# Float16 projection tiles of a hybrid decoder block: squares, scale sums and conversions issued a tile apart, and the last two raw tiles interleaved

## The chip, the cores and the metric

The kernel runs on one core of one Trainium2 chip. The metric is the device time of one execution in microseconds. Of the kernel before there are three timed runs, with a median of 2944.93 us, and one profiled execution.

## The reference, cut to what matters

```python
h = rms_norm(x, norm1_g)                 # x: 512 x 2048, float32
z = h @ w_in                             # w_in: 2048 rows; 72 tiles of up to 128 columns
zs = token_shift(z[..., :RW_SHIFT_COLS], rw_mu)
o_rw = rwkv7_mix(zs, ...)                # sequential over 512 tokens, 16 heads
o_att = swa_attention(q, k, v, ...)      # window 128, 16 query heads, 4 key heads
p = g_rw * (o_rw @ w_branch[:RW]) + g_att * (o_att @ w_branch[RW:])
x = x + p @ w_out
x = x + conv_ffn(rms_norm(x, norm2_g), w_up, conv_w, conv_b, w_down)
```

The change lies in `z = h @ w_in` and in what is interleaved with it. The rest, from `w_out` on, is not touched.

## The kernel before, in words

The output z is built transposed, one tile of 128 columns of `w_in` at a time: a tile is a sum over NK = 16 blocks of 128 input features, and each block takes three matmuls of 128x512 (high weight half times high input half, high times low, low times high), so 48 matmuls a tile. There are two kinds of tiles.

- **Raw tiles**, the first NR = 5 (two of keys, two of values, the first of queries). Their operands are float32r halves. `project` (L276) takes the 16 blocks in four groups of four. For each group `load_w` (L265) brings 256 KB of weights by a DMA on the SyncE queue into a tile of pool "raw" (four buffers), ScalarE writes the high half (`whi`, L271) and VectorE the low half (`wlo`, L272), four buffers each. The input halves are `xhi` and `xlo`, four tiles of four blocks each.
- **Float16 tiles**, the other 67. `zload(i)` (L357) brings the whole tile, 1 MB, in two DMAs, into one of four buffers that share their places with the four groups of `xhi` (tag "h1"); so the first four loads have to wait until the last raw tile has read a group for the last time. ScalarE squares each half and sums along the row (L367, output `zsq`, which takes two buffers of the same pool "raw"). `ztotal(i)` (L371) sums these over the partitions by two matmuls with one column each (L378) into the first column of the PSUM bank that tile i will accumulate in, and VectorE turns the sum into a power of two with four or five short instructions (L383 to L390). `zconv(i)` (L392) multiplies by it: ScalarE writes the high float16 half (`whi`, L402, two instructions a tile) and VectorE the low half (`wlo`, L403, two a tile), into the four buffers that the raw tiles use too. The 48 matmuls stand in L422. The float16 input `x16` is written by `row_scaled` (VectorE, L474) and `split` (ScalarE and VectorE, L220 and L221).

`ztile` (L406) puts these together. Before the change, tile i runs its matmuls, with `ztotal(i + 1)` after block 10 of 16; then come `zconv(i + 1)` and `zload(i + 5)`, whose squares are written right behind its DMAs.

Every engine works through its own queue in a fixed order. That order is made when the kernel is built: a list scheduler takes, on each engine, the earliest instruction in program order whose inputs it expects to be ready by its own estimate of durations. `behind(ins, other)` forces one instruction behind another on the same engine, and `pin` behind everything traced on that engine. Around the float16 tiles the program has three stages: attention (up to about 300 us), the start of the RWKV part (to about 405 us), and eight pairs of heads. In each pair the chain in `late(p)` (products of 64x64 blocks in L822 to L929, then eight steps of the scan in L936 to L949) is interleaved with six float16 tiles; `entries` ties some of its matmuls to places in the stream of tile matmuls. After about 1290 us come the products with `w_out`, `w_up` and `w_down` (L1176, L1312).

Of the kernel before, what the change touches and what calls it, by code (L numbers as in the profile page):

```python
# [19 lines left out]
P = 128  # L20
S = 512
# [114 lines left out]
def block_kernel(ctx: ExitStack, tc: tile.TileContext, d: Dims, a: dict, out: bass.AP):  # L136
    nc = tc.nc
    act, dve, pool, pe, sync = nc.scalar, nc.vector, nc.gpsimd, nc.tensor, nc.sync
    NK, NP, NQ, NKV, NF = d.NK, d.NP, d.NQ, d.NKV, d.NF
# [23 lines left out]
    cstp = abc.enter_context(tc.tile_pool(name="cstp", bufs=1))  # L163
    cst = cstp.tile([P, NCONST - P], F32, name="cst")
    mus = cstp.tile([P, 2, P], F32, name="mus")
    ones16 = cstp.tile([P, P], BF16, name="ones16")
    gsc = cstp.tile([P, 3], F32, name="gsc")
    xd = a["x"]
    GF = 4
    big1 = abc.enter_context(tc.tile_pool(name="big1", bufs=NK // GF, reuse_waits="tile"))  # L170
    wp = {"n": 0, "step": 3, "after": {}}
# [6 lines left out]
    x16 = x16p.tile([P, 2, NK, S], F16, name="x16")  # L178
# [4 lines left out]
    XG = 2  # L183
    xT = [px.tile([P, XG, S], F32, name=f"xT{i}") for i in range(NK // XG)]
# [34 lines left out]
    def split(hi, lo, src, pin=free):  # L219
        pin(act.activation(hi, src, AF.Copy))  # L220
        pin(dve.tensor_tensor(lo, src, hi.bitcast(F32) if hi.dtype == F32R else hi, op=ALU.subtract))  # L221
# [6 lines left out]
    for f in range(NPRE):  # L228
        w, t = a["w_up"][f], {n: up_d[f, n] for n in ("s3", "s1", "P6", "P3")}
# [19 lines left out]
    stream = []  # L249

    def behind(ins, before):
        tc.add_manual_dep(ins.ins, before.ins.name,
                          mybir.DependencyInfo(mybir.DependencyClass.NoSync, mybir.DependencyReason.DATA))
# [19 lines left out]
        background()  # L273
        return hi, lo

    def project(acc, src, xhi, xlo, pre=(), then=lambda i: None):  # L276
        nk = src.shape[1]
        for k0 in range(0, nk, 4):
            n = min(4, nk - k0)
            whi, wlo = pre[k0 // 4] if k0 // 4 < len(pre) else load_w(src[:, k0 : k0 + n])  # L280
            for j in range(n):
                k = k0 + j
                first, last = k == 0, k == nk - 1
                stream.append(pe.matmul(acc, whi[:, j], xhi(k), start=first, stop=False))  # L284
                stream.append(pe.matmul(acc, whi[:, j], xlo(k), start=False, stop=False))  # L285
                stream.append(pe.matmul(acc, wlo[:, j], xhi(k), start=False, stop=last))  # L286
            then(k0 // 4)


    id16 = cstp.tile([P, P], F16, name="id16")  # L290
# [6 lines left out]
    if True:  # L297
        xhi, xlo = by_group("xhi", "h1"), by_group("xlo", "l1")
        zt = {c: a["w_z"][i].rearrange("p (k c) -> p k c", c=P) for i, c in enumerate(d.z_tiles())}
# [4 lines left out]
        src = a["xT"].rearrange("p (k s) -> p k s", s=S)  # L304
        first = {d.c_ka: []}
# [27 lines left out]
        accp = pa.enter_context(tc.tile_pool(name="accA", bufs=3, space=PSUM, side="right", reuse_waits="tile"))  # L333

        zs = d.z_tiles()
        NR = 2 * NKV + 1
        at = 2 * NKV + NQ
        lead = at + 2 + d.GL // P + 3
        gated = [d.c_zr + i * P for i in range(2 * NK)]
        seq = zs[:at] + gated[:1] + zs[at:lead]  # L340
# [4 lines left out]
            used += GATES_PER_PAIR * NK // 16  # L345
        seq += gated[used:]
        zn = {"i": 0}
        Z = [{} for _ in seq]

        def mu_col(c0):  # L350
# [6 lines left out]
        def zload(i):  # L357
            if i >= len(seq):
                return
            raw = big1.tile([P, NK, P], F32, name="zraw", tag="h1")  # L360
            sums = cstp.tile([P, 2], F32, name="zsum", tag="zsum", bufs=4)
            Z[i].update(raw=raw, sums=sums)
            for h in range(2):
                ks = slice(h * NK // 2, (h + 1) * NK // 2)
                wp["last"] = sync.dma_start(raw[:, ks], zt[seq[i]][:, ks])
                sq = wp["raw"].tile([P, NK // 2, P], BF16, name="zsq", tag="raw")
                act.activation(sq, raw[:, ks], AF.Square, accum_out=sums[:, h : h + 1])  # L367
                for _ in range(2):
                    background()

        def ztotal(i):  # L371
            if i >= len(seq):
                return
            z = Z[i]
            z["acc"] = acc = accp.tile([P, S], F32, name="acc", tag="acc")
            part = z["sums"].bitcast(BF16)
            for h in range(2):
                ins = pe.matmul(acc[:, 0:1], ones16, part[:, 2 * h + 1 : 2 * h + 2], start=h == 0, stop=h == 1)  # L378
                behind(ins, stream[-1])
            q = cstp.tile([P, 1], I32, name="zq", tag="zq", bufs=2)  # L380
            zc = z["c"] = cstp.tile([P, 4], F32, name="zc", tag="zc", bufs=4)
            scale, back, e = zc[:, 0:1], zc[:, 1:2], zc[:, 2:4]
            dve.tensor_scalar(q, acc[:, 0:1].bitcast(I32), 24, None, op0=ALU.logical_shift_right)  # L383
            dve.tensor_scalar(scale.bitcast(I32), q, -(1 << 23), 204 << 23, op0=ALU.mult, op1=ALU.add)
            dve.tensor_scalar(back.bitcast(I32), q, 1 << 23, 50 << 23, op0=ALU.mult, op1=ALU.add)
            m = mu_col(seq[i])
            if m is not None:
                dve.tensor_scalar(e, mus[:, :, m], back, None, op0=ALU.mult)
            else:
                dve.tensor_scalar(e[:, 0:1], gsc[:, 1:2] if seq[i] < d.c_zr else gsc[:, 2:3], back, None, op0=ALU.mult)  # L390

        def zconv(i):  # L392
            if i >= len(seq):
                return
            z = Z[i]
            scale = z["c"][:, 0:1]
            raw = z.pop("raw")
            z["parts"] = []
            for h in range(2):
                src = raw[:, h * NK // 2 : (h + 1) * NK // 2]  # L400
                hi, lo = (wp["hl"].tile([P, NK // 2, P], F16, name=f"w{e}16", tag=f"w{e}") for e in ("hi", "lo"))
                act.activation(hi, src, AF.Copy, scale=scale)  # L402
                dve.scalar_tensor_tensor(lo, src, scale, hi, op0=ALU.mult, op1=ALU.subtract)  # L403
                z["parts"].append((hi, lo))

        def ztile(c0):  # L406
            i = zn["i"]
            zn["i"] += 1
            assert seq[i] == c0
            if i < NR:  # L410
                acc = accp.tile([P, S], F32, name="acc", tag="acc")
                last = i == NR - 1
                project(acc, zt[c0], xhi, xlo, first.pop(c0, ()), lambda g: zload(NR + g) if last else None)
                if last:
                    ztotal(NR)
            else:
                z = Z[i]
                acc, parts = z["acc"], z.pop("parts")
                for k in range(NK):
                    hi, lo = (x[:, k % (NK // 2)] for x in parts[2 * k // NK])  # L420
                    for w, e in ((hi, 0), (hi, 1), (lo, 0)):
                        stream.append(pe.matmul(acc, w, x16[:, e, k], start=k == 0 and e == 0 and w is hi,  # L422
                                                stop=k == NK - 1 and w is lo))
                    if k == 2 * NK // 3:
                        ztotal(i + 1)
                wp["e"] = z["c"][:, 2:4]
            if i >= NR - 1:
                zconv(i + 1)
                zload(i + 5)
            return acc  # L430

        acc_k = ztile(d.c_ka)
# [5 lines left out]
        with tc.tile_pool(name="x0_ps", bufs=1, space=PSUM) as ps0:  # L438
# [15 lines left out]
            q = p0.tile([P, 1], I32, name="gq")  # L454
# [17 lines left out]
        def row_scaled(k):  # L472
            x = xT[k // XG][:, k % XG]
            dve.scalar_tensor_tensor(x, x, n1s[:, k : k + 1], rowb, op0=ALU.mult, op1=ALU.mult)  # L474

        def scaled_halves():
            for k in range(NK):
                split(x16[:, 0, k], x16[:, 1, k], xT[k // XG][:, k % XG])
            xin.close()
            wp["gate"] = pa.enter_context(tc.tile_pool(name="gate", bufs=1, side="right"))  # L480
            wp["p"] = pt.enter_context(tc.tile_pool(name="attp", bufs=1, side="right", reuse_waits="tile"))
# [30 lines left out]
        with ExitStack() as pt:  # L512
# [59 lines left out]
            for t in range(1, NKV):  # L572
                for c0, then in ((d.c_ka, keys), (d.c_va, values)):
                    acc = ztile(c0 + t * P)
                    if spread:
                        behind(spread.pop(0), stream[-2 * NK - 1])
                        spread.clear()
                    todo.pop()()
                    todo.append(lambda acc=acc, then=then, t=t: then(acc, t))
                    for k in range(NK // 2) if then is keys else range(NK // 2, NK):  # L580
                        row_scaled(k)

            GQ = d.HQ // NHK

# [1088 lines left out]
```

## Time and profile before

| what | value |
|---|---|
| timed runs | 2940.71, 2944.93, 2949.1 us |
| profiled execution, time and span | 2952.12 us, 2950.3 us |
| busy shares of the span | PE 94%, PE weight loads 72%, VectorE 69%, ScalarE 50%, GpSimd 8% |
| mean granted TensorE clock | 0.977 |
| DMA traffic | 623.78 MB, 211 GB/s in the mean |

PE is TensorE's matmul side, PEld its weight load, DVE is VectorE, ACT is ScalarE, POOL is GpSimd, SP is SyncE and SPq its DMA queue. A row of a timeline gives the start in us, the duration in us, engine, line, operation, output and inputs, shapes and count; in square brackets stands how long the engine had been idle before it and what it waited for. A row of the waits gives the waiting engine and line, what it waited for, the total in us, the number of times and the longest. A row of stretches gives the length, then busy time and instructions of each engine, the granted clock, the DMA engines' share and GB/s.

### The profile page before, as it was taken

The page shows a single profiled execution, that of the slowest core. Times are in us where ns is not written, and L with a number is a line of the kernel's source. Part 1 is how long each engine was busy: PE and PEld are TensorE (multiplying, and loading weights), DVE is VectorE, ACT ScalarE, POOL GpSimd, SP SyncE. Part 2 cuts the span into 40 slices and gives each one's busy share as a digit, 9 for nine tenths or more (in the row PEclk, how much of TensorE's full clock was granted, in tenths as well). Part 3 has the DMA queues.
Part 4 walks back from the last instruction along what each step waited for, and adds up shares of the span by engine and source line. Part 5 has one row for each costly group of instructions (what it writes and reads, how often), then busy time and mean ns, then how long its engine had stood idle before and what let it go on. Part 6 is the DMA issues. An engine that isn't in the chain of part 4 may idle for free.

```text
span 2950.3 us, 45754 instructions
## 1 busy us (share of the span) xinstructions
PE 2776.3 (94%) x17547; PEld 2131.7 (72%) x17547; DVE 2034.1 (69%) x3621; ACT 1478.8 (50%) x2379; POOL 231.5 (8%) x309
## 2 busy tenths in 40 slices
PE   7788888988988989999999999999999999999999
PEld 6344345544544545468888999999999999888887
DVE  7378467677677677544567877778778777665555
ACT  6356454464454465432256655555554555544444
POOL 0000101100100100101100001011011110000000
PEclk9899999999999999999999999999999999999999
DMA  5654776866866766757877688888898887877775
GB/s 211 189 134 125 196 193 165 216 177 167 227 171 162 199 158 165 203 172 228 286 246 256 197 222 236 227 229 227 234 242 234 227 227 213 309 241 243 254 257 191
DMA packets 209035, 623.78 MB, mean 211 GB/s; under 512 B 22816, under 2 KB 42928, under 8 KB 207792
## 3 DMA queue, kind: packets, MB, share of 16 engines
q1 hardware_dynamic: 140256, 445.22, 45.2%
q0 software_dynamic: 37216, 136.33, 24.3%
q10 hardware_dynamic: 31344, 39.31, 3.8%
q8 instruction: 137, 2.24, 0.3%
q14 instruction: 82, 0.67, 0.1%
HBM read 571.16 MB, written 191.18 MB: 258 GB/s over the span
## 4 chain that ended last, share of the span: by engine, by line
PE 65%; DVE 12%; DMA 12%; ACT 6%; issue 3%; SPq 1%; POOL 0%; ACTq 0%; POOLq 0%; DVEq 0%
PE X L1312 17%; DMA zraw<-in_w_z_dram 10%; PE X L1176 9%; PE Y L1312 8%; PE Y L1176 8%; PE acc L422 7%; PE Z L1312 4%; DVE wlo L403 3%; PE acc L286 2%; PE acc L284 2%; PE acc L285 2%; ACT zsq L367 2%; ACT whi L402 2%; PE psS L945 1%; PE psG L936 1%
## 5 line engine op out<-in xcount | busy, mean ns | idle before, releaser
L422 PE MATMUL acc<-x,whi 128*128 128x512 f16 x2144 | 684.6, 391 | 25.6 <-ACT whi L402 21.9
L422 PE MATMUL acc<-x,wlo 128*128 128x512 f16 x1072 | 417.0, 389 | 11.7 <-DVE wlo L403 11.7
L1169 DVE TENSOR_TENSOR wlo<-raw,whi 128x1024 fp32r<-128x1024 f32 x210 | 256.7, 1224 | 199.9 <-ACT whi L1168 199.9
L422 PEld LDWEIGHTS <-whi 128*128 128x128 f16 x2144 | 208.4, 102 | 232.8 <-ACT whi L402 31.1
L1168 ACT ACTIVATE whi<-raw 128x1024 fp32r<-128x1024 f32 x210 | 222.6, 1061 | 281.5 <-PE X L1176 146.7
L1295 DVE TENSOR_TENSOR wlo<-raw,whi 128x1024 fp32r<-128x1024 f32 x184 | 224.6, 1222 | 77.7 <-ACT whi L1293 77.7
L1312 PE MATMUL X<-b,whi 128*128 128x256 f32 x1472 | 268.9, 283 | 0.2 <-ACT whi L1293 0.2
L1312 PE MATMUL X<-t,whi 128*128 128x256 f32 x1408 | 257.2, 283 | 1.4 <-ACT u L1340 1.4
L1312 PE MATMUL Y<-t,whi 128*128 128x256 f32 x1408 | 257.1, 283 | 0.0
L367 ACT ACTIVATE zsq<-zraw 128x1024 bf16<-128x1024 f32 x134 | 141.3, 1054 | 195.2 <-DMA zraw<-in_w_z_dram 194.1
L1293 ACT ACTIVATE whi<-a 128x1024 fp32r<-128x1024 f32 x124 | 130.9, 1056 | 200.8 <-DVE a L1288 197.2
L1312 PEld LDWEIGHTS X<-b,whi 128*128 128x128 f32 x1472 | 229.6, 192 | 0.4 <-ACT whi L1293 0.4
L1312 PEld LDWEIGHTS X<-t,whi 128*128 128x128 f32 x1408 | 219.6, 192 | 1.6 <-ACT u L1340 1.6
L1312 PEld LDWEIGHTS Y<-t,whi 128*128 128x128 f32 x1408 | 219.6, 192 | 0.0
L1312 PE MATMUL X<-b,wlo 128*128 128x256 f32 x736 | 208.6, 283 | 0.9 <-DVE wlo L1295 0.9
L422 PEld LDWEIGHTS <-wlo 128*128 128x128 f16 x1072 | 109.1, 102 | 133.3 <-DVE wlo L403 26.8
L403 DVE SCALAR_TENSOR_TENSOR wlo<-zraw,zc,whi 128x1024 f16<-128x1024 f32 x134 | 170.0, 1281 | 50.4 <-ACT whi L402 49.4
L1293 ACT ACTIVATE whi<-raw 128x1024 fp32r<-128x1024 f32 x184 | 193.0, 1049 | 22.8 <-ACT whi L1293 14.7
L1312 PE MATMUL X<-t,wlo 128*128 128x256 f32 x704 | 199.4, 283 | 0.5 <-DVE wlo L1295 0.5
L1312 PE MATMUL Y<-t,wlo 128*128 128x256 f32 x704 | 199.4, 283 | 0.2 <-DVE wlo L1295 0.2
L1295 DVE TENSOR_TENSOR wlo<-a,whi 128x1024 fp32r<-128x1024 f32 x124 | 151.9, 1225 | 67.6 <-ACT whi L1293 67.1
L1176 PE MATMUL X<-wlo,hhi 128*128 128x512 f32 x480 | 187.1, 390 | 0.8 <-DVE wlo L1169 0.8
(424 smaller groups left out, 5956.4 us busy)
## 6 DMA issues: line engine op xcount, KB each, us to landing
raw<-in_w_up_dram SPq DMA_DIRECT2D x170, 512.0 KB, 4.8
zraw<-in_w_z_dram SPq DMA_DIRECT2D x134, 512.0 KB, 5.8
s_dn<-in_w_dn_dram POOLq DMA_DIRECT2D x88, 512.0 KB, 6.4
raw<-s_dn SPq DMA_DIRECT2D x88, 512.0 KB, 3.9
raw<-in_w_up_dram POOLq DMA_DIRECT2D x80, 512.0 KB, 8.2
raw<-in_w_dn_dram SPq DMA_DIRECT2D x66, 512.0 KB, 3.7
s_dn<-in_w_dn_dram SPq DMA_DIRECT2D x44, 512.0 KB, 7.0
s_dn<-s_dn SPq DMA_DIRECT2D x44, 512.0 KB, 6.0
```

The costliest lines, as they stand in the source:

```text
L284: stream.append(pe.matmul(acc, whi[:, j], xhi(k), start=first, stop=False))
L285: stream.append(pe.matmul(acc, whi[:, j], xlo(k), start=False, stop=False))
L286: stream.append(pe.matmul(acc, wlo[:, j], xhi(k), start=False, stop=last))
L367: act.activation(sq, raw[:, ks], AF.Square, accum_out=sums[:, h : h + 1])
L403: dve.scalar_tensor_tensor(lo, src, scale, hi, op0=ALU.mult, op1=ALU.subtract)
L422: stream.append(pe.matmul(acc, w, x16[:, e, k], start=k == 0 and e == 0 and w is hi, stop=k == NK - 1 and w is lo))
L1168: act.activation(whi, wr, AF.Copy)
L1169: dve.tensor_tensor(wlo, wr, whi.bitcast(F32), op=ALU.subtract)
L1176: pe.matmul(dst, l[:, q, ts], r[:, es], start=fst and j == 0, stop=lst and j == 2, skip_group_check=True)
L1293: pin(act.activation(hi, t, AF.Copy))
L1295: return lambda: pin(dve.tensor_tensor(lo, t, hi.bitcast(F32), op=ALU.subtract))
L1312: pin(pe.matmul(ps, l[:, k], r[:, k], start=start and k + i == 0, stop=last and i == 2, skip_group_check=True))
```

## The change

- `zload` only loads. The squares become `zsquare(i)`, which is issued a tile before the sum needs it, and is forced behind the last conversion of the tile before (`behind(ins, after)`).
- `ztotal(i + 2)` comes at block 8 of tile i. Its column is put into the bank that tile i + 1 will accumulate in (column i % 2). `zconv(i + 2)`, then `zsquare(i + 3)` and `zload(i + 5)` follow at the end of tile i. So conversions are two tiles ahead of their matmuls where they were one ahead.
- The last two raw tiles (second value tile and first query tile) run together in `zpair`: group by group, first the one and then the other, and `zload(NR + g)` after group g of both. `zsquare(NR)` follows group 1; the sum and conversion of tile NR and the squares of NR + 1 stand ahead of group 3.
- `x16` is made pair of blocks by pair of blocks (128x1024) right behind `row_scaled`, ahead of those two raw tiles in program order; before it was made block by block behind the first query tile.

```diff
-    def project(acc, src, xhi, xlo, pre=(), then=lambda i: None):
+    def project(acc, src, xhi, xlo, pre=(), at=(0, 1)):
...
-                first, last = k == 0, k == nk - 1
+                first, last = k + at[0] == 0, k == nk - 1 and at[0] == at[1] - 1
...
-            then(k0 // 4)
...
         def zload(i):
...
-            raw = big1.tile([P, NK, P], F32, name="zraw", tag="h1")
-            sums = cstp.tile([P, 2], F32, name="zsum", tag="zsum", bufs=4)
-            Z[i].update(raw=raw, sums=sums)
+            raw = Z[i]["raw"] = big1.tile([P, NK, P], F32, name="zraw", tag="h1")
             for h in range(2):
                 ks = slice(h * NK // 2, (h + 1) * NK // 2)
                 wp["last"] = sync.dma_start(raw[:, ks], zt[seq[i]][:, ks])
-                sq = wp["raw"].tile([P, NK // 2, P], BF16, name="zsq", tag="raw")
-                act.activation(sq, raw[:, ks], AF.Square, accum_out=sums[:, h : h + 1])
                 for _ in range(2):
                     background()
 
-        def ztotal(i):
+        def zsquare(i, after=None):
+            if i >= len(seq):
+                return
+            raw = Z[i]["raw"]
+            sums = Z[i]["sums"] = cstp.tile([P, 2], F32, name="zsum", tag="zsum", bufs=4)
+            for h in range(2):
+                sq = wp["raw"].tile([P, NK // 2, P], BF16, name="zsq", tag="raw")
+                ins = act.activation(sq, raw[:, h * NK // 2 : (h + 1) * NK // 2], AF.Square, accum_out=sums[:, h : h + 1])
+                if after is not None:
+                    behind(ins, after)
+
+        def zacc(i):
+            if "acc" not in Z[i]:
+                Z[i]["acc"] = accp.tile([P, S], F32, name="acc", tag="acc")
+            return Z[i]["acc"]
+
+        def ztotal(i, bank):
...
-            z["acc"] = acc = accp.tile([P, S], F32, name="acc", tag="acc")
-            part = z["sums"].bitcast(BF16)
+            part, tot = z["sums"].bitcast(BF16), zacc(bank)[:, i % 2 : i % 2 + 1]
             for h in range(2):
-                ins = pe.matmul(acc[:, 0:1], ones16, part[:, 2 * h + 1 : 2 * h + 2], start=h == 0, stop=h == 1)
+                ins = pe.matmul(tot, ones16, part[:, 2 * h + 1 : 2 * h + 2], start=h == 0, stop=h == 1)
                 behind(ins, stream[-1])
...
-            dve.tensor_scalar(q, acc[:, 0:1].bitcast(I32), 24, None, op0=ALU.logical_shift_right)
+            dve.tensor_scalar(q, tot.bitcast(I32), 24, None, op0=ALU.logical_shift_right)
...
-                act.activation(hi, src, AF.Copy, scale=scale)
+                ins = act.activation(hi, src, AF.Copy, scale=scale)
                 dve.scalar_tensor_tensor(lo, src, scale, hi, op0=ALU.mult, op1=ALU.subtract)
                 z["parts"].append((hi, lo))
+            return ins
+
+        def zpair(tiles):
+            for g in range(NK // GF):
+                if g == NK // GF - 1:
+                    ztotal(NR, NR)
+                    at = zconv(NR)
+                    zsquare(NR + 1, at)
+                for acc, c0 in tiles:
+                    project(acc, zt[c0][:, g * GF : (g + 1) * GF], lambda k: xhi(g * GF + k), lambda k: xlo(g * GF + k),
+                            at=(g, NK // GF))
+                zload(NR + g)
+                if g == 1:
+                    zsquare(NR)
...
         def ztile(c0):
...
-                last = i == NR - 1
-                project(acc, zt[c0], xhi, xlo, first.pop(c0, ()), lambda g: zload(NR + g) if last else None)
-                if last:
-                    ztotal(NR)
-            else:
-                z = Z[i]
-                acc, parts = z["acc"], z.pop("parts")
-                for k in range(NK):
...
-                    if k == 2 * NK // 3:
-                        ztotal(i + 1)
-                wp["e"] = z["c"][:, 2:4]
-            if i >= NR - 1:
-                zconv(i + 1)
-                zload(i + 5)
+                if i < NR - 2:
+                    project(acc, zt[c0], xhi, xlo, first.pop(c0, ()))
+                else:
+                    held.append((acc, c0))
+                    if len(held) == 2:
+                        zpair(held)
+                return acc
+            if i == NR:
+                zload(NR + 4)
+            acc, parts = zacc(i), Z[i].pop("parts")
+            for k in range(NK):
...
+                if k == NK // 4 and i == NR:
+                    ztotal(NR + 1, NR + 1)
+                    zsquare(NR + 2, zconv(NR + 1))
+                if k == NK // 2:
+                    ztotal(i + 2, i + 1)
+            wp["e"] = Z[i]["c"][:, 2:4]
+            zsquare(i + 3, zconv(i + 2))
+            zload(i + 5)
             return acc
...
         def scaled_halves():
-            for k in range(NK):
-                split(x16[:, 0, k], x16[:, 1, k], xT[k // XG][:, k % XG])
...
                     for k in range(NK // 2) if then is keys else range(NK // 2, NK):
                         row_scaled(k)
+                        if k % XG == XG - 1:
+                            split(*(x16[:, e, k + 1 - XG : k + 1] for e in range(2)), xT[k // XG])
```

More of the change, by code (lines that the diff above doesn't have):

```diff
@@ L347, in block_kernel @@
         zn = {"i": 0}
+        held = []
         Z = [{} for _ in seq]
@@ L411, in ztile @@
                 acc = accp.tile([P, S], F32, name="acc", tag="acc")
-                last = i == NR - 1
-                project(acc, zt[c0], xhi, xlo, first.pop(c0, ()), lambda g: zload(NR + g) if last else None)
-                if last:
-                    ztotal(NR)
-            else:
-                z = Z[i]
-                acc, parts = z["acc"], z.pop("parts")
-                for k in range(NK):
[L420 to L423, printed above, removed]
-                    if k == 2 * NK // 3:
-                        ztotal(i + 1)
-                wp["e"] = z["c"][:, 2:4]
-            if i >= NR - 1:
-                zconv(i + 1)
-                zload(i + 5)
+                if i < NR - 2:
[9 more added lines that the diff above has]
+            for k in range(NK):
+                hi, lo = (x[:, k % (NK // 2)] for x in parts[2 * k // NK])
+                for w, e in ((hi, 0), (hi, 1), (lo, 0)):
+                    stream.append(pe.matmul(acc, w, x16[:, e, k], start=k == 0 and e == 0 and w is hi,
+                                            stop=k == NK - 1 and w is lo))
+                if k == NK // 4 and i == NR:
[6 more added lines that the diff above has]
+            zload(i + 5)
             return acc
```

## The prediction

> **What bounds the kernel now.** I read the page first, then stretches of time cut at the stages, then the waits of each stage, then timelines around the worst of them.
>
> ```profile
> PE 2776.3 (94%) x17547; PEld 2131.7 (72%) x17547; DVE 2034.1 (69%) x3621; ACT 1478.8 (50%) x2379; POOL 231.5 (8%) x309
> ```
>
> ```profile
> 62.00:104.00 42.00, 20.23 (x57) 14.07 (x56) 14.66 (x39) 9.48 (x18) 0.00 (x0) 0.67 0.34 113
> 104.00:135.00 31.00, 27.44 (x120) 11.91 (x120) 14.14 (x45) 12.72 (x19) 3.43 (x4) 0.89 0.86 248
> 135.00:300.00 165.00, 143.69 (x717) 74.42 (x718) 130.27 (x373) 91.54 (x238) 12.98 (x17) 0.97 0.52 139
> 300.00:405.00 105.00, 86.05 (x436) 40.72 (x434) 60.84 (x130) 52.50 (x87) 10.65 (x17) 0.96 0.70 186
> 405.00:1250.00 845.00, 759.46 (x5048) 417.21 (x5046) 587.05 (x1489) 448.18 (x876) 85.17 (x114) 0.96 0.70 185
> 1290.00:1440.00 150.00, 149.62 (x661) 122.75 (x660) 71.31 (x121) 36.58 (x60) 16.00 (x22) 1.00 0.79 238
> ```
>
> PE bounds everything. From 1290 us on it is full (149.6 of 150), and there nothing changes; time can only come out of PE's idle time before that: 21.8 us in 62 to 104, then 3.6, 21.3, 19.0 and 85.5, together 151 us. The waits, first ScalarE's longest of the whole run, then PE's in 300 to 405, then PE's in 405 to 1250:
>
> ```profile
> ACT zsq L367 <- DMA zraw<-in_w_z_dram: 194.1, 92, 11.0
> ```
>
> ```profile
> PE acc L422 <- ACT whi L402: 10.2, 4, 6.5
> PE acc L422 <- DVE wlo L403: 3.6, 6, 0.7
> ```
>
> ```profile
> PE bulk L873 <- DVE XIW L221: 34.2, 25, 3.7
> PE psS L945 <- DVE UV L941: 13.0, 9, 2.7
> PE acc L422 <- ACT whi L402: 8.7, 6, 1.5
> PE bulk L921 <- DVE XIW L917: 7.9, 10, 1.7
> PE acc L422 <- DVE wlo L403: 3.7, 11, 0.6
> ```
>
> ScalarE stood 194.1 us in front of squares whose tile had not landed, with all else in its queue behind them. PE stood in front of conversions (L402, L403) and of results of the chain.
>
> **The start, 50 to 105 us.** PE, SP's queue, ScalarE and PE again, from their timelines:
>
> ```profile
> 64.46 0.39 PE L285 MATMUL acc<-xlo,whi 128*128 128x512 f32 x1
> 64.69 0.39 PE L286 MATMUL acc<-xhi,wlo 128*128 128x512 f32 x1
> ```
>
> ```profile
> 65.11 0.83 SPq L365 DMA_DIRECT2D zraw<-in_w_z_dram  x2
> 66.04 0.36 SPq L268 DMA_DIRECT2D raw<-in_w_z_dram  x1
> ```
>
> ```profile
> 69.40 1.06 ACT L367 ACTIVATE zsq<-zraw 128x1024 bf16<-128x1024 f32 x1 [8.65 <-DMA zraw<-in_w_z_dram]
> ```
>
> ```profile
> 72.82 0.79 PE L284 MATMUL acc<-xhi,whi 128*128 128x512 f32 x1 [1.62 <-ACT whi L271]
> ...
> 105.17 0.60 PE L422 MATMUL acc<-x,whi 128*128 128x512 f16 x2
> ```
>
> The query tile's group 0 ends at 65.1 and its group 1 starts at 72.8: 7.7 us. Its weights were issued (66.04) only behind the tile load that had waited for the group's last read, and converted behind the squares of that load. This recurs at each of its groups. The clock granted in 62 to 104 was 0.67, so after a halt matmuls come about 0.4 us apart instead of 0.23 (64.46 to 64.69). By the Trainium skill ("TensorE: Matmul & The Clock Gate", Part 1) the clock halves after an idle window of some 3.4 us and returns after as much work: about 8 slow matmuls a halt, an estimate of 1.6 us each. By that rule the sum below would change by about 1 us; the 0.67 agrees with its direction.
>
> Interleaved, a group lasts 24 matmuls, 5.5 us, and the squares leave ScalarE's way. Two things stand against a full gain. The first is VectorE (then one row of ScalarE, and the landing time of the weights' DMA):
>
> ```profile
> 43.52 0.74 DVE L474 SCALAR_TENSOR_TENSOR xT<-xT,n1s,rowb 128x512 f32<-128x512 f32 x1
> ...
> 56.03 4.05 DVE L474 SCALAR_TENSOR_TENSOR xT<-xT,n1s,rowb 128x512 f32<-128x512 f32 x6
> 60.01 0.67 DVE L272 TENSOR_TENSOR wlo<-raw,whi 128x512 fp32r<-128x512 f32 x1
> 60.61 1.27 DVE L221 TENSOR_TENSOR x<-xT,x 128x512 f16<-128x512 f32 x2
> ```
>
> ```profile
> 52.52 0.63 ACT L271 ACTIVATE whi<-raw 128x512 fp32r<-128x512 f32 x1 [1.05 <-issue]
> ```
>
> ```profile
> raw<-in_w_z_dram SPq DMA_DIRECT2D x3, 256.0 KB, 5.1
> ```
>
> The `whi` done at 53.2 got its `wlo` only at 60.0: VectorE first took row scalings that stand earlier in the program, and the `x16` halves, which stand later, after it. In the new program all 16 scalings and all 8 paired `x16` low halves stand ahead of the pair's weights. From 43.5: 16 x 0.675 (4.05 / 6) = 10.8, 8 x 1.27 = 10.2, and an estimated 3 for key and value steps between: 67.5, and 0.67 for the delayed `wlo`: 68.2. Only the pair's very first `wlo` is made before the scalings begin. So PE, which starts the pair at about 49.8 (64.9 less 60 x 0.23 and 1.3 of small matmuls), runs one tile's group 0, halts from about 52.6 to 68.2, and ends group 0 with 10 matmuls at 0.4 at 72.3. Group 1, its weights long there: 5.5 and 1 for the clock, 78.8. Group 2: its buffers of pool "raw" are handed out behind the first squares, so its DMA goes out behind the first tile load, as all three did before: issued 73.2, landed 5.1 later, converted in 0.6 + 0.7: 79.6; end 86. Group 3: its buffers come behind the squares of NR + 1, and these behind a conversion behind a sum behind group 2; so its DMA goes out behind the third load: 7.7 us as before, 93.7, and 24 matmuls at a mean of 0.33: 101.6. Tile NR, converted meanwhile, starts there instead of at 105.2: **-4 us**. Best, without any of these halts: 49.8 + 22.1 + 2.6 of small matmuls = 74.5, that is -31. Worst, group 2's weights behind the second load too: 7 later, +3. I take -4, because the rows show buffers and VectorE following program order.
>
> **The float16 tiles.** Per tile there are the same two loads, squares, sums and conversions; only places change:
>
> ```profile
> L367 ACT ACTIVATE zsq<-zraw x134: 1039/1057/1067, 69.4 to 1235.7; 128x1024 bf16<-128x1024 f32 x134
> L367 ACT ACTIVATION_READ_ACCUMULATOR zsq<-zraw x134: 185/186/212, 70.4 to 1236.7; 128x1 f32 x134
> L402 ACT ACTIVATE whi<-zraw,zc x134: 1131/1136/1150, 104.0 to 1280.1; 128x1024 f16<-128x1024 f32 x134
> ```
>
> The squares of tile i + 3 come three tile ends after its load, so ScalarE's 194.1 us should vanish. On SP a load no longer waits for the conversion just ahead of it, and the background copies pinned behind the loads go no later. What late ScalarE and late conversions cost PE, first in the scan, then between a pair's first products:
>
> ```profile
> 589.68 1.06 ACT L367 ACTIVATE zsq<-zraw 128x1024 bf16<-128x1024 f32 x1 [3.87 <-DMA zraw<-in_w_z_dram]
> ```
>
> ```profile
> 591.25 1.12 PE L945 MATMUL psS<-UV,W 128*128 128x64 f32 x4 [2.46 <-DVE UV L941]
> ```
>
> ```profile
> 612.34 0.19 PE L378 MATMUL acc<-zsum,ones 128*128 128x1 bf16 x2
> ```
>
> ```profile
> 621.60 0.14 DVE L383 TENSOR_SCALAR zq<-acc 128x1 int32<-128x1 int32 x1
> ```
>
> ```profile
> 621.73 0.20 PE L873 MATMUL bulk<-XIW,BT 128*128 128x64 f16 x1 [3.04 <-DVE XIW L221]
> ...
> 624.00 1.03 PE L422 MATMUL acc<-x,whi 128*128 128x512 f16 x2 [1.51 <-ACT whi L402]
> ```
>
> Before 591 the scan waited for a copy that ScalarE could not make while it stood in front of a load. At 612.3 a sum was done, but VectorE, full of chain work, read it 9.3 us later; PE had neither chain nor tile.
>
> - 104 to 135: of 3.6 us idle those for conversions, and some of the slow clock (0.89): -3 (0 to -5).
> - 135 to 300, attention: 21.3 idle, most of it on the chain, which is freed from ScalarE's stalls in part: -5 (0 to -11).
> - 300 to 405: conversions 10.2 + 3.6 = 13.8 of 19.0, made a tile earlier now: -12 (0 to -16, with the clock).
> - 405 to 1250: conversions 8.7 + 3.7 = 12.4, of which -11. Scan 13.0: -10. Level products 34.2 + 7.9 = 42.1: halts like the 3.04 at 621.73, one in each of seven pairs, 21 us, stay, because the sum of tile i + 2 now sits in the bank of tile i + 1 and bars its first matmul until VectorE has read it; of the other 21 half, -10. Slow clock behind halts (two matmuls in 1.03 at 624.0): -2. Together -33 (0 to -50).
> - behind 1250, the last conversions: -2 (0 to -3).
>
> **New waits.** The sum of tile i + 2 needs squares that stand behind a conversion, which needs a buffer that PE frees at the end of tile i - 1. From there ScalarE needs 1.14 + 2 x (1.06 + 0.19) = 3.6 us; half a tile is 24 matmuls at 0.22 or so, 5.2. The slack is 1.6 us; chain work in ScalarE's queue can eat it, and then PE, in order, stands at the sum, with the chain's matmuls behind it. No row shows this wait; the nearest is PE's for ScalarE's conversions, 8.7 us. I take +8, with 0 and 67 tiles x 1.5 = 100 as ends.
>
> Sum: -4 - 3 - 5 - 12 - 33 - 2 + 8 = **-51 us** from the profiled execution's 2952.1 (span 2950.3): 2901. The median of the runs is 7.2 lower: **2894 us**. A difference of 0.3%, 9 us, is about what a measurement of this kernel can tell from none.
>
> **Rivals.**
> - *The start works in full.* If the pair's weights are there in time after all, it ends near 78 instead of 101.6: 2894 - 23 = 2871. For it: ScalarE and the DMA engines have room in 62 to 104 (9.48 of 42 us, a share of 0.34). Against: the `wlo` at 60.01.
> - *It doesn't do what it says.* The wait for the conversion is replaced by that for the bank: tiles start when VectorE has read the next sum, as late as at 621.60. Then the conversions' 25 and some 4 of clock and tail stay, and the start is at its bad end (+7): 2894 + 36, and with a reshuffled chain about 2935. For it: the 9.3 us behind 612.34. Against: the read is one short VectorE step, where the conversion needs three more on two engines.
> - *Slower: PE stands at the sums*, the wait of the last paragraph, in 67 tiles. It decides from (51 + 8) / 67 = 0.9 us a tile, that is with ScalarE 2.5 us late; at 1.5 it is 2894 - 8 + 100 = 2986. For it: the slack of 1.6. Against: the sum is placed where the squares are expected, and ScalarE is busy 448 of 845 us.
>
> **The numbers.** Forecast 0.55 (own range 2870 to 2920), full start 0.18, no real gain 0.15, slower 0.12. Faster: the first two, a third of the third and a little of the last, 0.79; same 0.09; slower 0.12. The range leaves out the slower case and the tails of the others: 2858 to 2945.
>
> **What would show it.** Right: no square waiting for `zraw`; L402 and L403 gone from PE's waits; scan waits (L945) under 4 us; PE idle in the pairs near 60 instead of 85.5; at the start one halt of some 15 us after the pair's first 12 matmuls and one of 8 ahead of its last group; the 3 us halts at L873 still there. Wrong: PE waiting at L378 for `zsum`, or at L422 for VectorE's L383, or a start without halts.

## The result, and the profile after

The changed kernel takes 2863.4 us (median of four runs, 2860.6 to 2869.3) where the kernel before took 2942.8 beside it: a ratio of 0.973 (95% interval 0.9707 to 0.9754), 79 us faster. The forecast was 2894 with a range of 2858 to 2945. Sign and mechanism came as forecast, the size was half as large again. The experiments below show that one of the four things that the change does earns nearly all of it, and that another one costs time.

The page after, first part, and its windows, cut at the same events as the windows of the kernel before that follow: the first float16 matmul, the first attention score product, the first product of the first pair's chain (L822 before, L852 after), the last float16 matmul. The columns are length, busy time of each engine, granted clock, DMA share.

```profile
PE 2747.2 (96%) x17547; PEld 2129.0 (74%) x17547; DVE 2032.1 (71%) x3613; ACT 1470.3 (51%) x2371; POOL 231.0 (8%) x309
```

```profile
50.00:96.00 46.00, 24.41 (x89) 18.60 (x88) 22.76 (x55) 12.76 (x17) 0.00 (x0) 0.74 0.27 83
96.00:145.50 49.50, 46.10 (x207) 23.45 (x207) 24.45 (x76) 20.68 (x31) 5.04 (x6) 0.90 0.97 279
145.50:350.40 204.90, 194.08 (x984) 98.14 (x984) 164.44 (x440) 127.17 (x292) 21.99 (x32) 0.99 0.65 182
350.40:1204.80 854.40, 795.92 (x5331) 443.71 (x5332) 626.35 (x1562) 474.10 (x932) 88.14 (x118) 0.98 0.71 189
```

```profile
50.00:105.20 55.20, 33.30 (x125) 25.09 (x124) 26.46 (x64) 18.92 (x33) 0.00 (x0) 0.75 0.30 97
105.20:146.90 41.70, 37.77 (x169) 16.22 (x169) 20.61 (x66) 16.17 (x23) 4.23 (x5) 0.92 0.84 245
146.90:378.10 231.20, 198.14 (x971) 99.01 (x971) 162.40 (x435) 122.67 (x285) 20.86 (x31) 0.96 0.58 156
378.10:1292.20 914.10, 819.44 (x5347) 445.60 (x5346) 630.21 (x1570) 482.94 (x935) 89.75 (x121) 0.96 0.68 180
```

The spans fell from 2950.3 to 2862.0, by 88.3 (the profiled execution before was 9 us above its median). Up to the first score product the gain is 1.4 us (146.9 to 145.5), from there to the chain 26.3, in the pairs 59.7, and behind them 1. PE did nearly the same number of matmuls in the pairs (5347 and 5331), yet its busy time fell by 23.5 us: they ran less often at the slow clock (0.96 to 0.98). The other 36 us there are idle time, 94.7 to 58.5.

The longest waits of PE up to 1230 us, after:

```profile
PE acc L450 <- DVE zq L394: 23.8, 9, 3.1
PE acc L284 <- ACT whi L271: 15.8, 3, 7.8
PE mi L528 <- DVE rq L211: 13.6, 6, 10.3
PE bulk L903 <- DVE XIW L221: 6.0, 18, 0.5
...
PE psS L975 <- DVE UV L971: 4.7, 21, 0.3
...
PE acc L389 <- ACT zsq L374: 2.4, 2, 2.1
```

The waits for conversions are down to two at the very start of tile NR (1.7 and 0.7 us), the scan's wait fell from 13.0 to 4.7, and ScalarE's wait for `zraw`, 194.1 us before, is down to one of 0.4. Its first square stood longer, but the profile names another DMA for it:

```profile
ACT zsq L374 <- DMA zraw<-in_w_z_dram: 0.4, 1, 0.4
```

```profile
79.13 1.06 ACT L374 ACTIVATE zsq<-zraw 128x1024 bf16<-128x1024 f32 x1 [11.86 <-DMA kd<-kn]
```

The load of that square's tile went out only at 74.00 (below), so a part of these 11.9 us can be a wait for it. There are two such waits, 16.9 us in all, both before 125 us; in the pairs no square waits for a load.

New at the top is PE's wait for `zq`, VectorE's reading of a sum: the halt of 3.1 us, in seven of the eight pairs, that stood at L873 before, now at the tile's own first matmul. PE, then VectorE, in the third pair:

```profile
557.77 0.19 PE L389 MATMUL acc<-zsum,ones 128*128 128x1 bf16 x2
...
572.87 1.01 PE L450 MATMUL acc<-x,whi 128*128 128x512 f16 x2 [3.09 <-DVE zq L394]
```

```profile
568.09 0.68 DVE L878 TENSOR_TENSOR BT<-AI,cst 128x512 f16<-128x512 f16 x1
...
572.68 0.14 DVE L394 TENSOR_SCALAR zq<-acc 128x1 int32<-128x1 int32 x1
```

The sum was done at 558; VectorE got to it at 572.68, behind a stretch of the chain's level work, and until then the next tile may not write its bank. At the start, PE's halts and then SP's queue:

```profile
68.74 0.38 PE L528 MATMUL mi<-ident,rq 128*8 128x128 f32 x1 [10.35 <-DVE rq L211]
...
86.08 0.80 PE L284 MATMUL acc<-xhi,whi 128*128 128x512 f32 x1 [6.89 <-ACT whi L271]
```

```profile
74.00 6.02 SPq L363 DMA_DIRECT2D zraw<-in_w_z_dram  x4
80.12 0.85 SPq L268 DMA_DIRECT2D raw<-in_w_z_dram  x2
```

VectorE's order holds the pair up as forecast, and the third group's weights go out behind two whole tile loads, not one.

### The profile page after: what moved, and what is told of

It is laid out like the page before. It is cut to its first block, busy times and chain, and to the rows that moved or that the text cites. A ratio compares the mean times of both kernels' runs of the same rounds, so it can differ in the third digit from the quotient of the medians.

```text
span 2862.0 us, 45787 instructions
## 1 busy us (share of the span) xinstructions
PE 2747.2 (96%) x17547; PEld 2129.0 (74%) x17547; DVE 2032.1 (71%) x3613; ACT 1470.3 (51%) x2371; POOL 231.0 (8%) x309
## 4 chain that ended last, share of the span: by engine, by line
PE 70%; DVE 15%; ACT 7%; DMA 5%; issue 3%; SPq 0%; POOL 0%; ACTq 0%; DVEq 0%; POOLq 0%
PE X L1342 17%; PE X L1206 10%; PE acc L450 9%; PE Y L1342 9%; PE Y L1206 9%; PE Z L1342 4%; DVE wlo L414 2%; PE acc L286 2%; PE acc L284 2%; PE acc L285 2%; ACT whi L413 2%; ACT zsq L374 2%; PE psS L975 1%; PE psG L966 1%; DVE tt L919 1%
## 5 line engine op out<-in xcount | busy, mean ns | idle before, releaser
L450 PE MATMUL acc<-x,whi 128*128 128x512 f16 x2144 | 664.5, 385 | 25.5 <-DVE zq L394 23.8
L450 PE MATMUL acc<-x,wlo 128*128 128x512 f16 x1072 | 412.2, 385 | 0.7 <-DVE wlo L414 0.7
L450 PEld LDWEIGHTS <-whi 128*128 128x128 f16 x2144 | 207.4, 100 | 231.9 <-issue 44.4
L413 ACT ACTIVATE whi<-zraw,zc 128x1024 f16<-128x1024 f32 x134 | 153.1, 1146 | 130.7 <-PE acc L450 61.2
L1323 ACT ACTIVATE whi<-raw 128x1024 fp32r<-128x1024 f32 x184 | 192.9, 1049 | 23.1 <-ACT whi L1323 13.9
L450 PEld LDWEIGHTS <-wlo 128*128 128x128 f16 x1072 | 108.3, 101 | 112.9 <-issue 12.3
```

The lines of the kernel that those rows point to most:

```text
L413: ins = act.activation(hi, src, AF.Copy, scale=scale)
L1323: pin(act.activation(hi, t, AF.Copy))
```

## The experiments

Theory at the outset: the gain comes from squares and conversions both being further apart, and the interleaved pair helps the start. Rival A: the squares' place alone is the loss. All versions beside the kernel before, median and ratio with interval; "first" is the time of the first float16 matmul, "per pair" the mean distance of two pairs' first chain products.

| version | us | ratio | first | per pair |
|---|---|---|---|---|
| before | 2942 to 2948 | 1 | 105.2 | 109.9 |
| changed | 2863.4 | 0.9730 (0.9707, 0.9754) | 96.0 | 102.9 |
| e1 squares apart only | 2846.0 | 0.9666 (0.9651, 0.9681) | 75.9 | 102.2 |
| e2 sums and conversions only | 2933.3 | 0.9958 (0.9944, 0.9973) | 104.7 | 109.3 |
| e3 both, no pair | 2839.7 | 0.9643 (0.9628, 0.9659) | 75.7 | 102.8 |
| e4 changed, `x16` halves behind | 2858.1 | 0.9707 (0.9692, 0.9722) | 88.9 | 102.6 |
| e5 changed, early sums | 2821.6 | 0.9578 (0.9548, 0.9607) | 94.0 | 100.3 |
| e6 = e3, early sums | 2803.0 | 0.9524 (0.9498, 0.9549) | 76.0 | 100.2 |
| e7 before, first four squares moved | 2914.1 | 0.9903 (0.9874, 0.9932) | 81.4 | 109.0 |
| e8 = e4, pair's weights ahead | 2846.4 | 0.9667 (0.9637, 0.9698) | 88.0 | 102.6 |
| e9 = e1, early sums | 2807.9 | 0.9543 (0.9517, 0.9568) | 75.7 | 101.4 |
| e10 = e6, squares not tied | 2884.5 | 0.9796 (0.9765, 0.9828) | 76.0 | 111.6 |

**e1, the squares apart, nothing else.** Sum and conversion stay one tile ahead, raw tiles and `x16` as before.

```diff
-                sq = ...; act.activation(sq, raw[:, ks], AF.Square, ...)     # in zload
+            at = zconv(i + 1)
+            zsquare(i + 3, at)          # behind the conversion; the first behind the last raw tile
             zload(i + 5)
```

> The kernel before with one part of the change: squares tied behind conversions and issued two tiles after their load; sums and conversions stay one tile ahead, raw tiles and x16 as before. My theory (both parts are needed, each for other waits): ScalarE's 194 us in front of zraw go, with them PE's scan waits (13.0 us) and half of the level waits; the conversion waits (33 us over the run) and the halt at the start of each pair stay, so also the slow clock behind it: some -35 us, about 2908. Rival A (squares waiting for DMAs were the whole loss): near the changed kernel, 2863 to 2875. Rival B (the distance of the conversions is the whole gain): 2935 to 2945.

2846.0: alone it earns 99 us, more than the whole change. The theory (about 2908) fell, and the time lies even below the 2863 to 2875 of Rival A. ScalarE's waits from 50 to 1300, the first two and that for `zraw`, of which 7.2 us are left, and then its start on SP's queue:

```profile
ACT UV L954 <- PE psU L953: 107.2, 48, 4.3
ACT whi L409 <- DVE zc L391: 90.9, 43, 6.7
...
ACT zsq L374 <- DMA zraw<-in_w_z_dram: 7.2, 1, 7.2
```

```profile
38.84 13.78 SPq L268 DMA_DIRECT2D raw<-in_w_z_dram  x7
...
65.17 3.52 SPq L363 DMA_DIRECT2D zraw<-in_w_z_dram  x4
```

The raw weights all go out before the first tile load. Before, the last three groups went out right behind tile loads (66.04 behind 65.11, 79.35 behind 78.44, 91.27 behind 90.38). With the squares written behind the raw tile, PE goes from 50 to 75.9 (25.9 us instead of 55.2) with one halt, of 1.9 us at its end, and with no interleaving at all. The place of the squares decides this: in e7 below, which moves nothing else, the raw weights go out first too. Whether the shared buffers of pool "raw" or the scheduler's estimates held them back was not tested.

**e2, sums and conversions two tiles ahead, squares at the loads.**

```diff
-                    if k == 2 * NK // 3:
-                        ztotal(i + 1)
+                    if k == NK // 2:
+                        ztotal(i + 2, i + 1)
...
-                zconv(i + 1)
+                zconv(i + 2)
```

> The kernel before with the other part: sums and conversions two tiles ahead, with the sum in the next tile's bank; squares stay right behind their DMAs, raw tiles and x16 as before. My theory: the conversion waits go and are partly replaced by waits for VectorE's read of the sum (about 3 us a pair), while ScalarE still stands in front of zraw (over 150 us) and the scan waits stay near 13: some -35 us, about 2908. Rival A: 2935 to 2945. Rival B: 2863 to 2875.

2933.3, 12 us, nearest to Rival A (2935 to 2945). ScalarE still stands, and the per-pair span hardly moves:

```profile
ACT zsq L367 <- DMA zraw<-in_w_z_dram: 184.3, 87, 10.1
```

The first chain product comes at 365.3 instead of 378.1: the 12.8 us are those of the stretch ahead of the chain. So the theory (about 2908) falls in this half too, and the squares' place is nearly the whole loss.

**e3, both, without the pair and with `x16` where it was.**

```diff
-                else:
-                    held.append((acc, c0))
-                    if len(held) == 2:
-                        zpair(held)          # project one after the other again, zload(NR + g) in the last
```

> Both parts of e1 and e2 together, without the interleaved pair and with x16 where it was. My theory: the pair and the moved x16 brought only about 1 us, since a halt of 16 us behind the delayed low half ate what the interleaving saved; so this is within 8 us of the changed kernel, 2855 to 2871, and the gains of e1 and e2 add up to it or to more. Rival (the pair carries a part of the gain): 10 to 25 us slower than the changed kernel, 2875 to 2890.

2839.7, 24 us faster than the changed kernel, outside what either side expected: the interleaved pair, with the moved `x16` halves, is a loss. First float16 matmul at 75.7 instead of 96.0, and the first score product at 114.5 instead of 145.5. Of that lead of 31.0 us 23.1 are left at the first chain product (327.3 against 350.4).

**e4, the changed kernel with the `x16` halves behind the first query tile again.**

```diff
         def scaled_halves():
+            for i in range(NK // XG):
+                split(*(x16[:, e, i * XG : (i + 1) * XG] for e in range(2)), xT[i])
```

> The changed kernel with the x16 halves written behind the first query tile again (still in pairs of blocks). My theory: the halt of 16 us after the pair's first 12 matmuls came from VectorE taking the x16 halves and scalings first. Without the halves ahead, the second tile's low half comes some 10 us earlier; the halts of 7 us in front of groups 2 and 4 stay: 8 to 12 us faster than the changed kernel, about 2853. Rival (the halt is the weights' DMA or ScalarE): no difference, 2860 to 2867.

2858.1: 5 us, between the theory (8 to 12) and the rival (none), and the intervals of the two ratios overlap. The halts of PE in its pair:

```profile
60.07 0.80 PE L286 MATMUL acc<-xhi,wlo 128*128 128x512 f32 x1 [5.21 <-DVE wlo L272]
80.12 0.79 PE L284 MATMUL acc<-xhi,whi 128*128 128x512 f32 x1 [9.67 <-ACT whi L271]
```

Half of the 10.35 us halt was VectorE's `x16` work; then the weights behind the loads cost more than before (9.67 for 6.89).

**e8, e4 with each group's weights fetched a group earlier.**

```diff
+            ahead = fetch(0)            # fetch(g): load_w of both tiles' group g
             for g in range(NK // GF):
+                ws, ahead = ahead, fetch(g + 1)
```

> The changed kernel with the x16 halves behind the first query tile as before (2858.1), and in the interleaved pair each group's raw weights fetched one group earlier, so that they stand ahead of the tile load and of the squares. Theory (the pair costs time only because its weights' transfers stand behind tile loads): no halt of PE over 3 us in the pair, first float16 matmul at 75 to 78 us, 2838 to 2845. Rival A (interleaving two raw tiles itself costs: 16 matmuls less between two uses of a buffer, or VectorE's low halves late): halts of 5 us stay at the pair's first groups, first float16 matmul at 82 to 90, 2850 to 2858.

2846.4. That lies between the theory's times and the rival's, 1.4 us above the theory's, but not by its picture: two halts stay and the first float16 matmul comes at 88.0, as rival A said.

```profile
60.02 0.79 PE L286 MATMUL acc<-xhi,wlo 128*128 128x512 f32 x1 [5.21 <-DVE wlo L272]
79.17 0.79 PE L284 MATMUL acc<-xhi,whi 128*128 128x512 f32 x1 [3.85 <-ACT whi L271]
```

The transfers behind the loads account for some 12 of the pair's 24 us; the `x16` halves for 5 (e4). The 7 us left to e3 go with the two halts, which e3 does not have: VectorE's low halves, which a pair needs twice as fast, and the last group's fetch, which still stands behind the second tile load (73.46 behind 72.79). They were not split further, and the intervals of the ratios of e8 and e3 overlap.

**e7, the kernel before with only its first four tiles' squares behind the raw tile.**

```diff
-                sq = ...; act.activation(sq, raw[:, ks], AF.Square, ...)
+                if i >= NR + 4:
+                    zsquare(raw, sums, h)
...
                 if last:
+                    ...                      # zsquare of tiles NR to NR + 3, not tied
                     ztotal(NR)
```

> The kernel before, with only the squares of the first four float16 tiles moved behind the query tile; all later squares stay at their loads. Theory (the start and the later tiles are two separate losses of the squares' place): the first float16 matmul comes at about 76 instead of 105 us, the per-pair span stays at 109 to 110 us, ScalarE still stands over 150 us in front of tiles that have not landed, and the time is 2913 to 2920, of the 99 us of the squares moved everywhere about 30. Rival (the start's gain is eaten by the attention stage, whose chain then waits): first float16 matmul at 76, but 2938 to 2945. Rival B (the early start also sets the later tiles' pace): under 2880.

2914.1 (0.9903): 28 us, as the theory said; its rivals fall. The first float16 matmul came at 81.4 instead of 76, since the first conversion (80.2) now stood behind six of the eight squares, three of which had waited for loads. ScalarE from 50 to 1300 still has

```profile
ACT zsq L359 <- DMA zraw<-in_w_z_dram: 162.1, 86, 7.2
```

and a pair takes 109.0. So of e1's 99 us some 28 are the start and 71 the later tiles.

**e6, e9, e5: the sum earlier.** In each the next sum stands in block 2 of a tile instead of block 8 (in e9, 10); e6 is e3 with it, e9 is e1, e5 the changed kernel. In e5 and e6 the squares are one tile further ahead, so that they are there.

```diff
-                if k == NK // 2:
+                if k == (NK // 2 if i == NR else 2):
                     ztotal(i + 2, i + 1)
...
-            zsquare(i + 3, zconv(i + 2))
+            zsquare(i + 4, zconv(i + 2))     # for i == NR, i + 3 as well
```

> The version without the interleaved pair (2839.7), with each float16 tile's sum made in block 2 of the tile before its neighbour instead of block 8, and the squares one more tile ahead so that they are there. Theory (the 3.1 us halt in each pair, 23.8 us in all, is PE barred from the next tile's bank until VectorE, busy with a stretch of chain work, has read the sum; earlier in the tile VectorE has time): the zq wait falls below 5 us and the time to 2812 to 2822. Rival A (VectorE's stretch is the cause, so PE only stands at the chain's own results, the level products, instead): the zq wait goes but XIW or UV waits grow by as much, 2835 to 2842. Rival B (PE now stands at the sums, for squares that are not made yet): a wait of PE at the sum's matmul of 20 us or more, 2850 or more.

> The version with the squares apart alone (2846.0; sum and conversions one tile ahead, each sum in its own tile's bank), with the sum in block 2 of the tile ahead instead of block 10. Theory (the 19.3 us of PE at the level products behind zc, and 10.5 us behind the conversions, come from the sum's place late in the tile, in front of a stretch of VectorE work): both fall to a few us, 2815 to 2825. Rival A (these products wait for XIW in truth, and zc is only named): the wait changes its name, 2840 to 2848. Rival B (a sum this early takes its bank before the tile two back has been read): PE stands at the sum, 2855 or more.

> The changed kernel itself (2863.4), with nothing but the sums in block 2 instead of block 8 and the squares one more tile ahead. Theory (PE's 3.1 us halt in each pair is a bank waiting for a sum that VectorE reads late; taking it away was worth 36.7 us without the interleaved pair, 26 of it more than the halts' own 10 to 24 because the matmuls behind a halt run slow): the zq wait under 5 us, slow matmuls behind 350 us from some 50 to under 10, and 2824 to 2832. Rival (the gain needs the start that the version without the pair has): 2840 to 2860.

2803.0, 2807.9 and 2821.6: each 35 to 45 us faster by the ratios than the version it is made from, and each below the range that the theory gave. PE's waits, e3 and then e6, from the chain's start on, and the windows of the same two:

```profile
PE acc L435 <- DVE zq L394: 23.4, 8, 3.1
PE bulk L892 <- DVE XIW L221: 6.3, 18, 0.7
```

```profile
PE bulk L895 <- DVE XIW L221: 8.0, 24, 0.6
PE bulk L999 <- DVE yc L992: 5.2, 8, 0.9
```

```profile
327.30:1181.40 854.10, 795.46 (x5331) 443.90 (x5332) 626.02 (x1562) 474.09 (x932) 88.06 (x118) 0.98 0.71 189
```

```profile
330.30:1138.50 808.20, 784.89 (x5330) 434.01 (x5331) 620.11 (x1553) 464.74 (x919) 88.01 (x118) 1.00 0.74 197
```

The `zq` wait is gone, and nothing has taken its place. Idle time falls from 58.6 to 23.3 us and busy time, at a clock of 1.00, by another 10.6. Of the 46 us of this window 8 come back behind it, where 1665.6 us are left instead of 1657.4. In e9 the level products' wait named `zc` (19.3 us in e1) falls to 0.4 in all, but the waits for conversions, which the theory saw at a few us, stay (8.9 and 5.4 us, 10.5 and 4.5 in e1): only half of its picture held. The sum's place, which the change did not improve, was worth half of what the change earned.

**e10, e6 without the order between squares and conversions.**

```diff
-                if after is not None:
-                    behind(ins, after)
```

> The version with early sums and without the pair (2803.0), without the explicit order of a tile's squares behind the conversions: their place in the program stays, and the scheduler puts them ahead of the conversions on ScalarE. Theory (what counts is that no square stands in ScalarE's queue before its tile has landed; a square one tile after its load, even ahead of a conversion, mostly finds it there): ScalarE's wait for zraw 10 to 60 us, per-pair span 100 to 102, 2803 to 2815. Rival (the tie is what keeps ScalarE free, without it the squares slide back to their loads): the wait over 120 us, slow matmuls back to 50 or more, 2830 to 2860.

2884.5: the theory fell, and the time is 24 us above even the rival's range; the tie is worth 80 us by the ratios. ScalarE and PE from 50 to 1300, and the pairs' window:

```profile
ACT zsq L374 <- DMA zraw<-in_w_z_dram: 151.5, 72, 7.2
```

```profile
PE bulk L893 <- DVE XIW L221: 28.6, 27, 3.3
PE bulk L941 <- DVE XIW L937: 22.7, 11, 6.6
```

```profile
340.60:1228.30 887.70, 808.03 (x5344) 444.04 (x5345) 620.96 (x1555) 470.57 (x919) 88.81 (x119) 0.97 0.68 179
```

The place in the program doesn't keep the squares behind their loads; the tie does. The likely reason: the scheduler places a square where it expects its data, ahead of the conversions, and the data come later than it expects, while with the tie the square stands behind a conversion that waits for PE (75.6 us in e6, 52 times), and by then the load has landed. This also is the cleanest test of the mechanism. One rule is taken from e6 (the scheduler may then have moved other instructions as well), and ScalarE's wait for `zraw` came back, and with it the waits for `XIW`, the slow clock and 80 us.

## Why the prediction was right, and where it was mis-sized

It named the right wait (ScalarE in front of squares that had not landed), the right stages and what would remain (a bank that waits for VectorE). Against its list: by the profile's names no square but one waits for `zraw` (0.4 us), the conversions are off PE's list in the pairs, PE's idle time there fell by 36.2 us to 58.5 (by 25 to near 60 was said, in a window 69 us shorter than that of before here), and PE stood at the sums for 2.4 us. One bound was missed narrowly: the scan waits 4.7 us, where under 4 was said. And one of its signs of being wrong came: PE waits at a tile's first matmul for VectorE's reading of the sum, 23.8 us. The text crosses itself there. Its sum had left 21 us for just this barred bank, but its list looked for them at L873; they moved to the tile's matmul and cost what the sum had left.

That the total came inside the range, 5 us from its fast end, is luck in part. It lies below the main case's own 2870 to 2920 and nearest to the 2871 of the full start, which did not happen: against the profiled spans the start fell 6 us short, while the stretch up to the chain gave 9 more than forecast and the rest 34 more.

- **The start and up to attention, -7 forecast, -1.4 measured.** The first halt (to 68.7 for 68.2) and the end of group 1 came as worked out. The step that failed is group 2: "issued 73.2", behind one load; it went out at 80.12 behind two, which the text had as its worst case; so the second halt (6.89 us) stood ahead of group 2. Tile NR then started at 96.0 ahead of the pair's last group, whose last matmul came at 108.4. The larger miss is one of cause: the step took VectorE's order and the buffers as things in which the pair runs short of its gain. e1 and e3 show 75.9 and 75.7 without a pair, 1.2 to 1.4 from the "best" (74.5) of the text, so the pair was what made the halts.
- **Attention and the start of the chain, -17 forecast, -26.3 measured.** The -12 for conversions is what e2 shows for the chain's start (12.8). But e1, with the conversions where they were, starts the chain at 332.9, and e3, with them further ahead, at 327.3: on top of the squares they bring 5.6 us here and nothing in the pairs (102.2 and 102.8 us a pair). Most of what the sum laid to the conversions' distance comes with the squares. Attention's -5 was too small: idle time from 146.9 to 378.1 went from 33.1 to 10.8.
- **The pairs and the tail, -35 and +8 forecast, -59.7 measured for the pairs and -0.9 behind them.** Idle time: scan 8.3 of the 10, level products 11.9 (42.1 to 6.0 + 0.8, and the 23.4 that moved to L450) of the 10 came as forecast. The wait at the sums was 2.4 in all, not 8. The term that failed is the slow clock, -2: measured, PE's busy time fell by 23.5 us. It counted a few matmuls behind the longest halts; but halts of 2 us slow PE as well, as the kernel before shows in its pairs:

```profile
806.18 0.59 PE L422 MATMUL acc<-x,whi 128*128 128x512 f16 x2
806.61 0.38 PE L422 MATMUL acc<-x,wlo 128*128 128x512 f16 x1
809.12 0.71 PE L945 MATMUL psS<-UV,W 128*128 128x64 f32 x4 [2.12 <-DVE UV L941]
809.62 1.06 PE L422 MATMUL acc<-x,whi 128*128 128x512 f16 x2
810.47 0.63 PE L422 MATMUL acc<-x,wlo 128*128 128x512 f16 x1
```

Behind 2.12 us of idle time two matmuls take 1.06 us instead of 0.59, and one 0.63 instead of 0.38. The whole amount could be estimated from the window: 819.44 us of matmuls at a granted clock of 0.96, so some 4% or 33 us; e6, run later, needs 784.89 for 5330 at 1.00, 34.6 us less.
- **Rivals.** That the bank's wait replaces the conversion's was real as a wait (23.8 us) but not as the outcome. The full start did not come in this kernel and came in e1 and e3. PE at the sums: 2.4 us.

So of the change's parts, the squares earn about 99 us (28 at the start, 71 later), sums and conversions two ahead 6 on top of them (e3 against e1; all four runs lie below, but the intervals of the ratios overlap a little), and the pair with the moved `x16` halves costs 24.

## What to carry to other kernels

Look for an instruction that stands in an in-order queue in front of a transfer, with other work behind it: ScalarE was only half busy, and moving 134 short squares behind work that is late for another reason was worth 3.3%. If a scheduler orders the queue by its own estimates, tie the order; the place in the program alone did not hold. A one-column read that guards a bank belongs as early as its input allows, and once a queue is free, an interleaving meant to hide its stalls has to be tried again without: e6, with early sums and no pair, takes 2803.0 us, 0.9524 (0.9498 to 0.9549) of the kernel before, and is the fastest version here, with e9 (2807.9, conversions one tile ahead) inside its interval.

## What the runs showed of the hardware

The price of a halt is more than its length. From e3 to e6 eight halts of up to 3.1 us went, 23.4 us by the list of waits; the busy time of the same matmuls fell by 10.6 as well, an estimate of 1.3 us a halt if all of it is laid to these eight. The prediction's estimate from the Trainium skill ("TensorE: Matmul & The Clock Gate", Part 1) was 1.6 us a halt, so the price is near. What was underestimated is the number of halts that pay. Three stretches of the kernel before around the halt of 2.12 us above (length, busy times, granted clock):

```profile
806.19:809.60 3.41, 1.28 (x8) 0.67 (x7) 1.23 (x3) 1.26 (x3) 0.00 (x0) 1.00 1.02 404
809.60:813.01 3.41, 3.41 (x10) 1.23 (x10) 2.57 (x6) 1.76 (x3) 1.62 (x2) 0.50 0.85 168
813.01:816.42 3.41, 3.41 (x19) 1.61 (x18) 2.78 (x10) 2.20 (x3) 0.00 (x0) 1.00 1.09 209
```

PE worked for 1.28 of 3.41 us in the first stretch and without a pause in the second, which was granted half the clock. The same page of the Trainium skill sets the idle window at about 3.4 us; here a stretch of that length with 1.28 us of work in it was enough.
